# Scores, softmax, transposes and values of two sets of attention tiles as one chain that goes in step

## The chip, the core and the metric

The kernel runs on one core of a Trainium2 chip. The metric is the device time of one execution in microseconds (us), as the median of several executions. The core's engines run side by side, each through its own list of instructions in order: TensorE (PE in the profile, its weight loads PEld), VectorE (DVE), ScalarE (ACT), GpSimdE (POOL) and SyncE (SP), which here issues nearly all DMA commands. They wait for each other by semaphores.

## What is computed

One encoder layer for two sequences with the same weights: A with 1024 rows and B with 512, 1024 features each. All is float32.

```python
u = rmsnorm(x, norm1_g) * (1.0 + sc1) + sh1
z = u @ w_in
z_hy, q, k, v, g = jnp.split(z, ...)
y_hy = hyena_branch(z_hy, ...)        # x0 * long_conv(x1 * v, filter): FFT length 2L
y_at = dilated_attention(q, k, v, ...)
mixed = (g_hy * (y_hy @ w_hy_br) + g_at * (y_at @ w_at_br)) @ w_out
h = x + gt1 * mixed
ff = jnp.square(jax.nn.relu(u2 @ w_up)) @ w_down      # u2: h normalised and modulated
return h + gt2 * ff
```

The shifts, scales and gates (`sh1`, `sc1`, `gt1` and three more) come from a small product with `ada_w`, the modulation. Attention has three groups of four heads of 64 features. A group of dilation 1, 4 or 16 splits the sequence into as many interleaved sub-sequences; a query sees the keys within 64 places on both sides there:

```python
s = jnp.einsum('...bqd,...bkd->...bqk', qb, kw)
s = jnp.where(valid, s + bias, NEG_INF)
m = jnp.max(s, axis=-1, keepdims=True)
p = jnp.exp(s - m)
den = jnp.sum(p, axis=-1, keepdims=True)
o = jnp.einsum('...bqk,...bkd->...bqd', p, vw) / den
lse = (m + jnp.log(den))[..., 0]
```

The three groups' outputs are then merged with weights `softmax(lse)` over the groups.

## The kernel before, in words

**The main stream.** All large products go through `mm3` (matmul on L770): a weight tile of 128 columns against 128 x 512 pieces of the activations, each float32 operand split into a high and a low part, with three products of the parts. Such a product is a *unit*: 48 matmuls for A, 24 for B. `stream` runs the units one after the other: qkv of group 0, zhy (the input of the convolution) third by third mixed with qkv of groups 1 and 2, gates; then the same for B; then the output products (mixA, mixB) and the MLP (ffA, ffB). For each unit the next unit's weights are split (L401 on ACT, L402 on DVE), and a unit's result is evicted from PSUM, for zhy by L1054 on ACT and L1055 and L1056 on DVE. Main products have two PSUM buffers (`psm`); all side work shares four (`pss`).

**Side work.** Everything else is written as generators, *sides*: filters (`filtA`, `filtB`), long convolutions (`conv_gen`, one per third of the channels: L953, L966, a trip through DRAM by L969 and L933, L996, the product with the filter's spectrum, L1007, another trip, L1032), attention (`att_gen`, one per group), the merging of the groups (`combine_gen`, products on L1366), the rest of the modulation (`ada_rest`, L638) and the normalisation of B. A side yields a cost and a latency. After every few main matmuls `pump` adds their cost to a virtual clock and advances whichever started side is ready by it, until the budget, cost times a ratio, is used up. `par` runs several chains of one side together, each with a ready time of its own. So the place of an instruction is decided when the program is built, by numbers, not on the chip. Then a scheduler orders PE, DVE, POOL and SP; ACT keeps the written order. `ada_rest` starts when the three convolutions of A have ended.

**Attention.** `att_gen` waits until q, k and v of its group are there, loads the bias (L1412) and then works tile by tile, a tile being 128 queries. `chain(tiles)` treats one tile, or two where all keys of a tile are 128 (group 2 of A, groups 1 and 2 of B). It has four steps with a yield behind each: scores (L1255 on PE, then scale plus bias L1261 and the row maximum L1264 on DVE), exponentials (L1271 on ACT, with row sums), transposes (L1280 on PE, and the copy of the result by L388), values (L1290 on PE, and a copy into the output). Latencies after the first three are `LSM` = 4.0, `LEX` = 2.5 and `LPT` = 2.5. The chains ran through `par([...], WA)` with `WA` = 2: two at a time, each at its own pace, and a new one is begun when one is done.

## Time and profile before

| | |
|---|---|
| median of 3 runs | 2611.21 us (2610.47 to 2611.28) |
| profiled execution | 2608.41 us, span 2606.6 us |
| granted TensorE clock, mean | 0.996 |
| PE busy | 2551.0 us (98%), 12872 instructions |
| DVE, ACT, POOL busy | 48%, 33%, 6% |

Stages of the profiled execution, roughly: qkv, zhy and gates of A to 849 us, qkv and zhy and gates of B to 1254, mixing of A and B to 1556, MLP of A to 2254 and of B to the end. Attention runs beside the main stream between some 130 and 1130 us. In the profile, a wait is put down to the semaphore event that came last. A row of a timeline gives start, duration, engine, line, operation, output and inputs (numbers of buffers left out), shape and, in brackets, the idle time before it and what ended it.

### The profile page before, as it was taken

How to read it: one execution, taken by the hardware profiler on the slowest of the kernel's cores; microseconds unless marked ns; L12 is line 12 of the kernel's file. 1: busy time of each engine (PE TensorE's matmuls, PEld its weight loads, DVE VectorE, ACT ScalarE, POOL GpSimd, SP SyncE). 2: the span in 40 equal slices, each digit the busy share in tenths (PEclk: the TensorE clock that was granted, in tenths of full speed). 3: DMA queues.
4: the chain of work that ended last, by engine and by line, in shares of the span. 5: the costliest groups of instructions: out<-in, count | busy, mean ns of one | idle time of the engine just before them, and what ended most of it. 6: DMA issues, size and time to landing. Idle time of an engine off the chain costs nothing.

```text
span 2606.6 us, 31910 instructions
## 1 busy us (share of the span) xinstructions
PE 2551.0 (98%) x12872; PEld 2051.2 (79%) x12872; DVE 1249.3 (48%) x1626; ACT 861.3 (33%) x1398; POOL 152.0 (6%) x122
## 2 busy tenths in 40 slices
PE   8999999999999899999999989999999999999999
PEld 4677788787888577787788868888888888888887
DVE  4354443744557745653545563333333333554544
ACT  5544323532522454443432442111211121323232
POOL 0111000000010210000122210000000000000000
PEclk9999999999999999999999999999999999999999
DMA  7455575556665354556754531111111112332323
GB/s 270 142 161 186 178 189 169 152 177 163 210 216 196 131 160 138 160 157 214 249 181 139 170 110 49 42 49 55 49 41 48 57 49 73 130 104 90 103 91 105
DMA packets 136953, 348.95 MB, mean 134 GB/s; under 512 B 18888, under 2 KB 50175, under 8 KB 136678
## 3 DMA queue, kind: packets, MB, share of 16 engines
q1 hardware_dynamic: 136518, 346.13, 41.0%
q8 instruction: 102, 1.67, 0.3%
q0 software_dynamic: 288, 0.79, 0.1%
q14 instruction: 45, 0.37, 0.0%
HBM read 278.58 MB, written 71.16 MB: 134 GB/s over the span
## 4 chain that ended last, share of the span: by engine, by line
PE 69%; DVE 2%; DMA 1%; ACT 1%; issue 1%; POOL 0%; SPq 0%; DVEq 0%; ACTq 0%; POOLq 0%
PE ffA__mm L770 27%; PE ffB__mm L770 13%; PE gateA__mm L770 7%; PE mixA__mm L770 6%; PE zhyB__mm L770 4%; PE qkvB__mm L770 3%; PE mixB__mm L770 2%; PE gateB__mm L770 2%; PE filtB__s L901 0%; DVE mixB__wl L402 0%; PE convB__s L1007 0%; DMA convB__g<-convB__dr 0%; PE attB__s L1290 0%; DMA mixA__g<-zhyA__dr 0%; PE convB__s L996 0%
## 5 line engine op out<-in xcount | busy, mean ns | idle before, releaser
L770 PE MATMUL ffA__mm<-ffA__g,ffA__wh 128*128 128x512 f32 x1024 | 274.1, 389 | 0.0
L770 PE MATMUL ffA__mm<-normA__g,ffA__wh 128*128 128x512 f32 x992 | 265.1, 389 | 0.0
L770 PEld LDWEIGHTS ffA__mm<-ffA__g,ffA__wh 128*128 128x128 f32 x1024 | 192.0, 188 | 40.5 <-issue 0.4
L770 PEld LDWEIGHTS ffA__mm<-normA__g,ffA__wh 128*128 128x128 f32 x992 | 186.2, 188 | 38.7
L1545 DVE SCALAR_TENSOR_TENSOR mixA__g<-ffA__mm,adam,mixA__g 128x1024 f32<-128x1024 f32 x64 | 82.1, 1283 | 190.0 <-PE ffA__mm L770 190.0
L770 PE MATMUL ffB__mm<-ffB__g,ffB__wh 128*128 128x512 f32 x512 | 157.8, 389 | 0.0
L770 PE MATMUL ffA__mm<-ffA__g,ffA__wl 128*128 128x512 f32 x512 | 157.7, 389 | 0.0
L770 PE MATMUL ffB__mm<-normB__g,ffB__wh 128*128 128x512 f32 x496 | 152.7, 389 | 0.0
L770 PE MATMUL ffA__mm<-normA__g,ffA__wl 128*128 128x512 f32 x496 | 152.7, 389 | 0.0
L401 ACT CAST ffA__wh<-ffA__wr 128x1024 fp32r<-128x1024 f32 x63 | 66.3, 1052 | 256.6 <-PE ffA__mm L770 213.6
L1527 DVE SCALAR_TENSOR_TENSOR ffA__g<-ffA__mm,ffA__g 128x1024 f32<-128x1024 f32 x32 | 39.2, 1225 | 222.7 <-ACT ffA__g L1526 222.7
L770 PE MATMUL zhyA__mm<-init__g,zhyA__wh 128*128 128x512 f32 x512 | 145.2, 400 | 0.0
L770 PE MATMUL gateA__mm<-init__g,gateA__wh 128*128 128x512 f32 x480 | 132.0, 394 | 0.0
L770 PE MATMUL mixA__mm<-mixA__g,mixA__wh 128*128 128x512 f32 x424 | 115.3, 392 | 3.1 <-DVE mixA__g L1479 1.9
L770 PE MATMUL qkvA__mm<-init__g,qkvA__wh 128*128 128x512 f32 x416 | 117.0, 399 | 0.0
L770 PEld LDWEIGHTS zhyA__mm<-init__g,zhyA__wh 128*128 128x128 f32 x512 | 94.2, 188 | 23.6 <-issue 5.7
L770 PEld LDWEIGHTS ffB__mm<-ffB__g,ffB__wh 128*128 128x128 f32 x512 | 96.0, 188 | 20.2 <-ACT ffB__g L401 0.2
L770 PEld LDWEIGHTS ffA__mm<-ffA__g,ffA__wl 128*128 128x128 f32 x512 | 96.1, 188 | 20.0
L1526 ACT ACTIVATE ffA__g<-ffA__mm 128x1024 f32<-128x1024 f32 x32 | 32.9, 1029 | 237.7 <-PE ffA__mm L770 237.7
L770 PEld LDWEIGHTS ffA__mm<-normA__g,ffA__wl 128*128 128x128 f32 x496 | 93.1, 188 | 19.3
L770 PEld LDWEIGHTS ffB__mm<-normB__g,ffB__wh 128*128 128x128 f32 x496 | 93.1, 188 | 19.3
L770 PEld LDWEIGHTS gateA__mm<-init__g,gateA__wh 128*128 128x128 f32 x480 | 89.5, 188 | 20.2 <-issue 1.3
(499 smaller groups left out, 4910.4 us busy)
## 6 DMA issues: line engine op xcount, KB each, us to landing
ada__g<-ada SPq DMA_DIRECT2D x32, 512.0 KB
ffA__wr<-w_up SPq DMA_DIRECT2D x32, 512.0 KB
ffA__wr<-w_dn SPq DMA_DIRECT2D x32, 512.0 KB
ffB__wr<-w_dn SPq DMA_DIRECT2D x32, 512.0 KB
ffB__wr<-w_up SPq DMA_DIRECT2D x30, 512.0 KB
filtA__dr<-filtA__g SPq DMA_DIRECT2D x24, 512.0 KB
convA__g<-filtA__dr SPq DMA_DIRECT2D x48, 256.0 KB
init__g<-ada SPq DMA_DIRECT2D x16, 512.0 KB
```

The lines of the kernel that those rows point to most:

```text
L401: A.copy(hi, raw)
L770: T.matmul(ps[:, 512 * c:512 * c + 512], ww[:, sl], xx(k)[:, 512 * c:512 * c + 512], start=k == 0 and p == 0, stop=k == kt - 1 and p == 2)
L1526: A.activation(r, ps[:, :L], AF.Relu)
L1527: V.scalar_tensor_tensor(r, ps[:, :L], 0.0, r, ALU.max, ALU.mult)
L1545: V.scalar_tensor_tensor(S.h(m), ps[:, :L], mod(S, 5, m), S.h(m), ALU.mult, ALU.add)
```

## The change

`chain` now takes two sets of tiles, *parts*, at once. Scores of both are computed, then DVE evaluates both, then the exponentials of both, the transposes part by part, and the values of both. Each step yields the sum of the parts' costs; the latencies behind scores and exponentials are doubled, that behind the transposes stays. `par` is gone here: the next chain begins when the last one has ended. All instructions are the same in number and shape; lines after L1240 move by 17 (L1255 becomes L1264, L1261 L1271, L1264 L1274, L1271 L1283, L1280 L1293, L1290 L1305, L1366 L1383).

```diff
@@ -1237,67 +1237,84 @@
             return k0, k1, [(t0 - k0, n if n < 128 else min(n, k1 - t0), vv) for t0, n, vv in vts if k0 <= t0 < k1]
-        def chain(tiles):
-            k = {i: keys(i) for i in tiles}
-            nk = k[tiles[0]][1] - k[tiles[0]][0]
-            np_ = len(k[tiles[0]][2])
-            w = 256 // len(tiles)
-            slots = [(a, f, i) for a, (i, f) in enumerate((i, f) for i in tiles for f in range(2))]
-            ps = [pss().rearrange("p (a b) -> p a b", b=w) for _ in range(2)]
-            s = [sp.tile([128, 512 // w, w], F32, tag="sc", name=nm("sc"), bufs=4) for _ in range(2)]
-            pieces = k[tiles[0]][2]
-            full = max(o for o, _, _ in pieces) + 128
-            for t in s if full > nk else ():
-                G_.memset(t[:, :, nk:full], 0.0)
-            for a, f, i in slots:
-                k0, k1, _ = k[i]
+
+        class Part:
+            pass
+
+        def chain(parts):
+            subs = []
+            for tiles in parts:
+                c = Part()
+                subs.append(c)
+                c.tiles = tiles
+                c.k = {i: keys(i) for i in tiles}
+                c.pieces = c.k[tiles[0]][2]
+                c.nk = c.k[tiles[0]][1] - c.k[tiles[0]][0]
+                c.np = len(c.pieces)
+                w = 256 // len(tiles)
+                c.slots = [(a, f, i) for a, (i, f) in enumerate((i, f) for i in tiles for f in range(2))]
+                c.ps = [pss().rearrange("p (a b) -> p a b", b=w) for _ in range(2)]
+                c.s = [sp.tile([128, 512 // w, w], F32, tag="sc", name=nm("sc"), bufs=4) for _ in range(2)]
+                full = max(o for o, _, _ in c.pieces) + 128
+                for t in c.s if full > c.nk else ():
+                    G_.memset(t[:, :, c.nk:full], 0.0)
+                for a, f, i in c.slots:
+                    k0, k1, _ = c.k[i]
+                    for hh in range(2):
+                        T.matmul(c.ps[hh][:, a, :c.nk], q(f)[64 * hh:64 * hh + 64, 128 * i:128 * i + 128],
+                                 kx(f)[64 * hh:64 * hh + 64, k0:k1], start=True, stop=True)
+            for c in subs:
                 for hh in range(2):
-                    T.matmul(ps[hh][:, a, :nk], q(f)[64 * hh:64 * hh + 64, 128 * i:128 * i + 128],
-                             kx(f)[64 * hh:64 * hh + 64, k0:k1], start=True, stop=True)
-            for hh in range(2):
-                for a, f, i in slots:
-                    h, k0 = 2 * f + hh, k[i][0]
-                    o = (k0 - 128 * i + 64, k0 - 128 * i + 128, 0)[gi] - x0
-                    V.scalar_tensor_tensor(s[hh][:, a, :nk], ps[hh][:, a, :nk], rq[:, 2 * hh + f, i:i + 1],
-                                           bias[h][:, o:o + nk], ALU.mult, ALU.add)
-                for b, i in enumerate(tiles):
-                    V.tensor_reduce(st[:, i, 2 * hh:2 * hh + 2], s[hh][:, 2 * b:2 * b + 2, :nk], AX.X, ALU.max,
-                                    negate=True)
-            yield 0.0034 * nk * len(tiles) + 0.3, LSM
-            table(LN_EXP)
-            for hh in range(2):
-                for a, f, i in slots:
-                    sl = 2 * hh + f
-                    A.activation(s[hh][:, a, :nk], s[hh][:, a, :nk], AF.Exp, bias=st[:, i, sl:sl + 1],
-                                 accum_out=st[:, i, 4 + sl:5 + sl])
-            yield 0.0, LEX
-            pT = []
-            for hh in range(2):
-                pt = pss().rearrange("p (a b) -> p a b", a=4)
-                pT.append(sp.tile([128, 4, 128], F32, tag="pT", name=nm("pT"), bufs=4))
-                for a, f, i in slots:
-                    for j, (o, _, _) in enumerate(k[i][2]):
-                        T.transpose(pt[:, a * np_ + j], s[hh][:, a, o:o + 128], ident)
-                na = len(slots) * np_
-                copy(pT[hh][:, :na], pt[:, :na])
-            yield 0.22 * np_ * len(slots), LPT
-            po = pss().rearrange("p (a b) -> p a b", a=4)
-            for b, i in enumerate(tiles):
+                    for a, f, i in c.slots:
+                        h, k0 = 2 * f + hh, c.k[i][0]
+                        o = (k0 - 128 * i + 64, k0 - 128 * i + 128, 0)[gi] - x0
+                        V.scalar_tensor_tensor(c.s[hh][:, a, :c.nk], c.ps[hh][:, a, :c.nk],
+                                               rq[:, 2 * hh + f, i:i + 1], bias[h][:, o:o + c.nk], ALU.mult, ALU.add)
+                    for b, i in enumerate(c.tiles):
+                        V.tensor_reduce(st[:, i, 2 * hh:2 * hh + 2], c.s[hh][:, 2 * b:2 * b + 2, :c.nk], AX.X,
+                                        ALU.max, negate=True)
+                del c.ps
+            yield sum(0.0034 * c.nk * len(c.tiles) + 0.3 for c in subs), LSM * len(subs)
+            for c in subs:
+                table(LN_EXP)
                 for hh in range(2):
-                    for j, (_, _, vv) in enumerate(k[i][2]):
-                        for f in range(2):
-                            h = 2 * f + hh
-                            T.matmul(po[64 * f:64 * f + 64, 2 * b + hh], vv[:, 64 * h:64 * h + 64],
-                                     pT[hh][:, (2 * b + f) * np_ + j], start=j == 0, stop=j == np_ - 1)
-            for b, i in enumerate(tiles):
-                n0 = 128 * i
-                t0 = n0 % per * dil + n0 // per
+                    for a, f, i in c.slots:
+                        sl = 2 * hh + f
+                        A.activation(c.s[hh][:, a, :c.nk], c.s[hh][:, a, :c.nk], AF.Exp, bias=st[:, i, sl:sl + 1],
+                                     accum_out=st[:, i, 4 + sl:5 + sl])
+            yield 0.0, LEX * len(subs)
+            for c in subs:
+                c.pT = []
                 for hh in range(2):
-                    copy(O(hh)[:, t0:t0 + 127 * dil + 1:dil], po[:, 2 * b + hh])
-            yield 0.45 * np_ * len(tiles) + 0.3, 0.0
+                    pt = pss().rearrange("p (a b) -> p a b", a=4)
+                    c.pT.append(sp.tile([128, 4, 128], F32, tag="pT", name=nm("pT"), bufs=4))
+                    for a, f, i in c.slots:
+                        for j, (o, _, _) in enumerate(c.k[i][2]):
+                            T.transpose(pt[:, a * c.np + j], c.s[hh][:, a, o:o + 128], ident)
+                    na = len(c.slots) * c.np
+                    copy(c.pT[hh][:, :na], pt[:, :na])
+                yield 0.22 * c.np * len(c.slots), 0.0
+            yield 0.0, LPT
+            for c in subs:
+                c.po = pss().rearrange("p (a b) -> p a b", a=4)
+                for b, i in enumerate(c.tiles):
+                    for hh in range(2):
+                        for j, (_, _, vv) in enumerate(c.k[i][2]):
+                            for f in range(2):
+                                h = 2 * f + hh
+                                T.matmul(c.po[64 * f:64 * f + 64, 2 * b + hh], vv[:, 64 * h:64 * h + 64],
+                                         c.pT[hh][:, (2 * b + f) * c.np + j], start=j == 0, stop=j == c.np - 1)
+            for c in subs:
+                for b, i in enumerate(c.tiles):
+                    n0 = 128 * i
+                    t0 = n0 % per * dil + n0 // per
+                    for hh in range(2):
+                        copy(O(hh)[:, t0:t0 + 127 * dil + 1:dil], c.po[:, 2 * b + hh])
+            yield sum(0.45 * c.np * len(c.tiles) + 0.3 for c in subs), 0.0
         many = 2 if keys(0)[1] == 128 else 1
-        yield from par([chain(range(i, i + many)) for i in range(0, nt, many)], WA)
+        for n in range(0, nt, 2 * many):
+            yield from chain([range(i, i + many) for i in range(n, min(n + 2 * many, nt), many)])
         att_on.remove(gi)
         S.O[gi], S.st[gi] = O, st
```

How the order of instructions moves, at three places. First PE, where conv A's second third (L996, L1007) meets the first tiles of attention's group 1 in A. The names `convA__s` and `attA__s` are results in PSUM. Before:

```order
L996 MATMUL convA__s_3727<-convA__g_3642,convA__cm_3654 128x256 x2
L996 MATMUL convA__s_3734<-convA__g_3642,convA__cm_3654 128x256 x2
L1280 MATMUL attA__s_3772<-csq,attA__sc_3691 128x128 x4
L770 MATMUL zhyA__mm_3755<-init__g_434,zhyA__wh_3592 128x512 x2
L770 MATMUL zhyA__mm_3755<-init__g_430,zhyA__wl_3593 128x512 x2
L1280 MATMUL attA__s_3779<-csq,attA__sc_3692 128x128 x4
L1280 MATMUL attA__s_3792<-csq,attA__sc_3707 128x128 x4
L1280 MATMUL attA__s_3799<-csq,attA__sc_3708 128x128 x4
L1007 MATMUL convA__s_3813<-convA__g_3725,convA__cm_3656 128x256 x2
L1007 MATMUL convA__s_3817<-convA__g_3725,convA__cm_3656 128x256 x2
```

Now:

```order
L1188 MATMUL qkvA__s_3652<-csq,qkvA__g_3605 128x128
L996 MATMUL convA__s_3673<-convA__g_3583,convA__cm_3595 128x256 x2
L996 MATMUL convA__s_3680<-convA__g_3583,convA__cm_3595 128x256 x2
L1264 MATMUL attA__s_3693<-qkvA__g_3371,qkvA__g_3004 128x192
L1264 MATMUL attA__s_3694<-qkvA__g_3371,qkvA__g_3004 128x192
...
L770 MATMUL zhyA__mm_3775<-init__g_253,zhyA__wl_3610 128x512
L1264 MATMUL attA__s_3703<-qkvA__g_3371,qkvA__g_3004 128x256
...
L1007 MATMUL convA__s_3736<-convA__g_3671,convA__cm_3597 128x256 x2
L770 MATMUL zhyA__mm_3775<-init__g_320,zhyA__wh_3609 128x512 x2
L1007 MATMUL convA__s_3740<-convA__g_3671,convA__cm_3597 128x256 x2
```

Before, the last L966 stood 63 main matmuls ahead of the first L996, now 26. The first scores of the group now stand between L996 and L1007, and their transposes (L1293, not in these rows) come 36 to 48 main matmuls behind them, where before transposes (L1280) stood between L996 and L1007.

Second DVE, at the merging of A's groups (L1366, now L1383), which stands beside the start of B's filter and the modulation's multiplies (L638). Before:

```order
L1366 TENSOR_TENSOR attA__g_1375<-combineA__s_7020,attA__g_1375 128x512
L795 TENSOR_SCALAR filtB__g_7001<-filtB__g_7000 128x256
L654 TENSOR_TENSOR qkvB__smt_6973<-qkvB__sma_6971,qkvB__smy_6972 128x16
L638 ISA ada__g_7017,adam<-ada__g_6951,ada__g_5670,prm 128x1024
L638 ISA adam 128x1
L796 TENSOR_SCALAR filtB__g_7001<-filtB__g_7001 128x256
L655 SCALAR_TENSOR_TENSOR qkvB__smt_6973<-qkvB__smt_6973,qkvB__smy_6972 128x16
L638 ISA ada__g_7017,adam<-ada__g_6951,ada__g_5671,prm 128x1024
L638 ISA adam 128x1
L1366 TENSOR_TENSOR attA__g_3845<-combineA__s_7023,attA__g_3845 128x512
```

Now:

```order
L638 ISA ada__g_6897,adam<-ada__g_6822,ada__g_5507,prm 128x1024
L638 ISA adam 128x1
...
L402 TENSOR_TENSOR qkvB__wl_6915<-qkvB__g_6776,qkvB__wh_6914 128x1024
...
L1383 TENSOR_TENSOR attA__g_1450<-combineA__s_6981,attA__g_1450 128x512
...
L1383 TENSOR_TENSOR attA__g_1450<-combineA__s_7022,attA__g_1450 128x512
L795 TENSOR_SCALAR filtB__g_7006<-filtB__g_7005 128x256
L654 TENSOR_TENSOR qkvB__smt_6978<-qkvB__sma_6976,qkvB__smy_6977 128x16
L1383 TENSOR_TENSOR attA__g_3894<-combineA__s_7025,attA__g_3894 128x512
L1383 TENSOR_TENSOR attA__g_5616<-combineA__s_7028,attA__g_5616 128x512
```

The last of the multiplies (L638) stood between merge products; now it stands ahead of all of them, and the merge products of the second piece alternate with rows of the filter.

Third DVE, at group 2 of attention in B; L1055, L1056 and L402 are the main stream's eviction and weight split. Before:

```order
L1055 SCALAR_TENSOR_TENSOR zhyB__g_9011<-zhyB__mm_8933,prm,zhyB__g_9011 128x511
L1261 SCALAR_TENSOR_TENSOR attB__sc_8989<-attB__s_8987,qkvB__rq_7742,attB__g_8941 128x128 x4
L1264 TENSOR_REDUCE attB__st_8940<-attB__sc_8989 128x2 x2
L1261 SCALAR_TENSOR_TENSOR attB__sc_8990<-attB__s_8988,qkvB__rq_7742,attB__g_8941 128x128 x4
L1264 TENSOR_REDUCE attB__st_8940<-attB__sc_8990 128x2 x2
L1056 SCALAR_TENSOR_TENSOR zhyB__g_9011<-zhyB__mm_8933,prm,zhyB__g_9011 128x511
L402 TENSOR_TENSOR zhyB__wl_9018<-zhyB__g_8864,zhyB__wh_9017 128x1024
L1261 SCALAR_TENSOR_TENSOR attB__sc_9036<-attB__s_9034,qkvB__rq_7742,attB__g_8941 128x128 x4
L1264 TENSOR_REDUCE attB__st_8940<-attB__sc_9036 128x2 x2
L1261 SCALAR_TENSOR_TENSOR attB__sc_9037<-attB__s_9035,qkvB__rq_7742,attB__g_8941 128x128 x4
L1264 TENSOR_REDUCE attB__st_8940<-attB__sc_9037 128x2 x2
```

Now:

```order
L1055 SCALAR_TENSOR_TENSOR zhyB__g_9023<-zhyB__mm_8932,prm,zhyB__g_9023 128x511
L1271 SCALAR_TENSOR_TENSOR attB__sc_8977<-attB__s_8975,qkvB__rq_7757,attB__g_8941 128x128 x3
L1274 TENSOR_REDUCE attB__st_8940<-attB__sc_8977 128x2 x2
L1271 SCALAR_TENSOR_TENSOR attB__sc_8978<-attB__s_8976,qkvB__rq_7757,attB__g_8941 128x128 x3
L1274 TENSOR_REDUCE attB__st_8940<-attB__sc_8978 128x2 x2
L1271 SCALAR_TENSOR_TENSOR attB__sc_8989<-attB__s_8987,qkvB__rq_7757,attB__g_8941 128x128 x4
L1274 TENSOR_REDUCE attB__st_8940<-attB__sc_8989 128x2 x2
L1271 SCALAR_TENSOR_TENSOR attB__sc_8990<-attB__s_8988,qkvB__rq_7757,attB__g_8941 128x128 x4
L1274 TENSOR_REDUCE attB__st_8940<-attB__sc_8990 128x2 x2
L1056 SCALAR_TENSOR_TENSOR zhyB__g_9023<-zhyB__mm_8932,prm,zhyB__g_9023 128x511
L402 TENSOR_TENSOR zhyB__wl_9030<-zhyB__g_8880,zhyB__wh_9029 128x1024
```

Each pair of score tiles (L1261 and L1264, now L1271 and L1274) was a group of its own with an eviction and a split between; now the four score tiles of both parts stand between L1055 and L1056 of the same unit.

## The prediction

> **What bounds the kernel now.** I read the page's busy times and chain first, then the matrix engine's waits, then windows and timelines where these waits lie.
>
> ```profile
> PE 2551.0 (98%) x12872; PEld 2051.2 (79%) x12872; DVE 1249.3 (48%) x1626; ACT 861.3 (33%) x1398; POOL 152.0 (6%) x122
> PE 69%; DVE 2%; DMA 1%; ACT 1%; issue 1%; POOL 0%; SPq 0%; DVEq 0%; ACTq 0%; POOLq 0%
> ```
>
> PE is busy for 98% of the span, and its work also makes the chain that ended last. The change issues the same matmuls, so it can win only from the idle 2%, from the gaps between kinds of matmul, and from the clock. The waits of PE that lie near attention, convolution and merging (time in all, count, longest):
>
> ```profile
> PE combineA__s L1364 <- DVE attA__g L1366: 5.4, 2, 3.5
> PE convB__s L1032 <- DMA convB__g<-convB__dr: 2.5, 1, 2.5
> PE qkvB__s L664 <- DVE attA__g L1366: 1.9, 1, 1.9
> PE attA__s L1280 <- ACT attA__sc L1271: 1.7, 1, 1.7
> PE attA__s L1280 <- DVE convA__g L999: 1.7, 1, 1.7
> PE convB__s L996 <- DMA convB__g<-convB__dr: 1.5, 1, 1.5
> ```
>
> Only two of the six name attention's own chain (L1280), 3.4 us together, and the second of them is held by a convolution's product. The others belong to work whose place the change shifts. The windows around three of these places (window, length, busy PE, PEld, DVE, ACT, POOL, granted clock, DMA share, GB/s):
>
> ```profile
> 463.00:475.00 12.00, 8.47 (x48) 6.02 (x48) 11.30 (x17) 8.91 (x24) 0.41 (x2) 0.86 0.17 46
> 877.00:891.00 14.00, 6.55 (x17) 3.01 (x17) 12.70 (x26) 4.80 (x9) 5.63 (x5) 0.75 0.33 112
> 891.00:896.00 5.00, 4.81 (x16) 3.50 (x15) 2.90 (x3) 2.93 (x5) 3.65 (x4) 0.68 0.31 105
> ```
>
> In the first two DVE is busy nearly throughout and PE is not: there DVE's order sets the end. The third has a busy PE at a clock of 0.68.
>
> **The change, part by part.** All matmuls, score passes, exponentials, copies and DMA issues stay; no tile grows. Terms below are in us of the profiled execution.
>
> *Fewer changes between kinds of matmul.* A values or score block stands between streams of main matmuls:
>
> ```profile
> 160.45 0.61 PE L770 MATMUL zhyA__mm<-init__g,zhyA__wl 128*128 128x512 f32 x2
> 161.00 1.97 PE L1290 MATMUL attA__s<-attA__pT,qkvA__g 128*64 128x128 f32 x32
> 163.92 2.58 PE L1255 MATMUL attA__s<-qkvA__g,qkvA__g 64*128 64x256 f32 x16
> 166.43 1.20 PE L770 MATMUL zhyA__mm<-init__g,zhyA__wh 128*128 128x512 f32 x4
> 167.46 0.62 PE L770 MATMUL zhyA__mm<-init__g,zhyA__wl 128*128 128x512 f32 x2
> 167.92 1.09 PE L770 MATMUL zhyA__mm<-init__g,zhyA__wh 128*128 128x512 f32 x4
> ```
>
> Two main matmuls take 0.46 start to start (167.46 to 167.92), thus 0.23 each; before the values block they take 0.55, so 0.09 is lost going in, and the first four after the score block take 1.03 instead of 0.92, so 0.11 coming out. Counted in the order of instructions, PE passes between array shapes 193 times before and 171 times after, since blocks of the two parts now touch: 22 x 0.09 = **-2.0**. Ends: -2.4 (22 x 0.11) and 0, if a block's own first matmul hides it.
>
> *Start of group 1 in A, beside conv A's second third.* Before:
>
> ```profile
> 443.82 0.28 PE L966 MATMUL convA__s<-convA__g,f1ul 128*128 128x256 f32 x1
> 458.77 0.28 DVE L986 COPY convA__g<-convA__g 1x256 f32<-1x256 f32 x1 [10.68 <-DMA convA__g<-filtA__dr]
> 460.09 0.27 DVE L988 MEMSET convA__g<- 1x256 f32 x1 [0.65 <-DMA convA__g<-filtA__dr]
> 467.69 0.93 PE L1280 MATMUL attA__s<-csq,attA__sc 128*128 128x128 f32 x4 [1.75 <-ACT attA__sc L1271]
> 470.34 0.63 PE L1280 MATMUL attA__s<-csq,attA__sc 128*128 128x128 f32 x4 [1.73 <-DVE convA__g L999]
> 470.81 3.50 PE L1007 MATMUL convA__s<-convA__g,convA__cm 128*128 128x256 f32 x8
> ```
>
> The stretch loses 1.75 + 1.73 waiting and some 1.6 in slow matmuls of L1007 (3.50 for eight, where L996 takes 1.89 for eight below). Afterwards L1280's transposes come 36 to 48 main matmuls behind their scores, so both waits and that clock loss go: -5.1. But the convolution's second step (L996) moves from 63 main matmuls behind the last L966 to 26, and the third (L1007) to 40. What its data needs:
>
> ```profile
> 577.89 0.29 PE L966 MATMUL convA__s<-convA__g,f1ul 128*128 128x256 f32 x1
> 588.03 1.89 PE L996 MATMUL convA__s<-convA__g,convA__cm 128*128 128x256 f32 x8
> 1201.07 0.28 PE L966 MATMUL convB__s<-convB__g,f1ul 128*128 128x256 f32 x1
> 1211.64 1.10 PE L996 MATMUL convB__s<-convB__g,convB__cm 128*128 128x256 f32 x4 [1.50 <-DMA convB__g<-convB__dr]
> ```
>
> In A's last third L996 followed after 588.03 - 578.18 = 9.85 with no wait (an upper bound for the way through memory), in B it waited and came after 10.3. Now 26 x 0.23 = 6.0 plus sixteen V transposes (some 1.9) give 7.9: a wait of 0 to 2.4, I take 1.8. Then the product needs the filter spectrum, which DVE got at 460.09, 16.0 after the last L966; L1007 now stands some 13 behind it (40 x 0.23, the transposes, L996, a score block), so it waits for 3 and the product's own length: 4.5 with some clock loss. Together -5.1 + 1.8 + 4.5 = **+1.2**. Ends: -5.1 (loads land earlier, as SP issues them sooner behind the same L969) and +6 (a product of 3 behind it and a clock as at 470.81). Behind a DVE that waits at L986 stand the score passes of both parts and the eviction and weight split of the main stream (L1055, L402).
>
> *Convolution B.* L1032's wait of 2.5 lies behind 25 main matmuls and now 51: 26 more are 6.0, so it goes, **-2.5** (ends -2.5, 0). In its last third L996 moves from 56 to 36 behind L966: 8.3 against 10.3, **+2.0** (0 to 2.7). Conv A's first third goes from 49 to 42: 9.7 against 9.85, **+0.3** (0 to 1.7).
>
> *Group 0 in A.* At one place sixteen transposes and both parts' values now stand without main matmuls between. The copies between them, at the like place before:
>
> ```profile
> 157.04 2.05 ACT L388 COPY attA__pT<-attA__s 128x512 f32<-128x512 f32 x4 [1.67 <-PE attA__s L1280]
> ```
>
> Four copies take 2.05 and the sixteen transposes less, so the second values block waits for about the difference: **+0.7**; ends 0 and 3 (a cast and exponentials queued ahead of the copies).
>
> *The merging of A's groups (L1366, now L1383).* Before:
>
> ```profile
> 879.15 1.28 DVE L638 CUSTOM_DVE_ANT_0 ada__g<-ada__g,ada__g,prm 128x1024 f32<-128x1024 f32 x1
> 880.65 1.28 DVE L638 CUSTOM_DVE_ANT_0 ada__g<-ada__g,ada__g,prm 128x1024 f32<-128x1024 f32 x1
> 882.27 0.68 DVE L1366 TENSOR_TENSOR attA__g<-combineA__s,attA__g 128x512 f32<-128x512 f32 x1
> 883.01 0.49 PE L1364 MATMUL combineA__s<-combineA__g,combineA__g 128*128 128x512 f32 x1 [3.50 <-DVE attA__g L1366]
> 885.37 1.99 PE L1364 MATMUL combineA__s<-combineA__g,combineA__g 128*128 128x512 f32 x3 [1.86 <-DVE attA__g L1366]
> 889.26 1.07 PE L664 MATMUL qkvB__s<-qkvB__g,csq 128*32 128x256 f32 x4 [1.91 <-DVE attA__g L1366]
> 890.26 1.22 PE L770 MATMUL qkvB__mm<-normB__g,qkvB__wh 128*128 128x512 f32 x2
> ```
>
> Of the wait of 3.50, 2 x 1.28 = 2.6 are two multiplies of the modulation (L638) that stand in DVE's order ahead of the product PE waits for. In the new order the last of them stands some fifteen rows before the first merge product, because conv A ends 19 main matmuls (4.3) earlier and that work starts earlier. Also, main matmuls now lie between the merging ones, 11 where 9 merging matmuls stood together: up to 2.5 of cover. 2.6 + about 1.9 of the 2.5 = **-4.5**. Ends: all three waits and the slow clock of 891 to 896, 7.3 + 0.32 x 5 = -8.9; and 0, if the multiplies only stall PE at an earlier place.
>
> [...]
>
> *Bursts in B.* The scores of both parts are now evaluated in one run of DVE:
>
> ```profile
> 1105.56 1.12 DVE L1261 SCALAR_TENSOR_TENSOR attB__sc<-attB__s,qkvB__rq,attB__g 128x128 f32<-128x128 f32 x4
> 1106.59 0.73 DVE L1264 TENSOR_REDUCE attB__st<-attB__sc 128x2 f32<-128x256 f32 x2
> 1108.92 0.74 DVE L1056 SCALAR_TENSOR_TENSOR zhyB__g<-zhyB__mm,prm,zhyB__g 128x511 f32<-128x511 f32 x1
> 1109.58 1.21 DVE L402 TENSOR_TENSOR zhyB__wl<-zhyB__g,zhyB__wh 128x1024 fp32r<-128x1024 f32 x1
> ```
>
> Before, one part (two such pairs, 1108.92 - 1105.56 = 3.4) stood ahead of L1056 and L402; now it is both, 6.8. A unit of B is 24 main matmuls, 5.5, so up to 1.4 of the burst shows in a unit: 1.4 and half of it in another group, **+2.1**. Ends 0 (started early in the unit) and 5 (2 x 1.4 and the split behind it twice, 1.2 each).
>
> *Costed at nothing.* The exponentials of both parts now stand in one row on ACT, whose order is as written:
>
> ```profile
> 151.54 0.45 ACT L1271 ACTIVATE attA__sc<-attA__sc,attA__st 128x192 f32<-128x192 f32 x1
> ```
>
> The second part's four (eight in B) put off the main eviction and cast behind them by at least 4 x 0.45 = 1.8 (3.6). A unit of A lasts 48 x 0.23 = 11 and ACT is busy for a third of the span, so main work covers it; without that cover it costs those 1.8 at each burst that meets an eviction, which the ends of the bursts' and of group 0's terms take in. The chain issues no DMA of its own; its fills on POOL (6% busy) move with the scores, and on SP the bias loads of a group stand behind the convolution's spectrum loads (L984) in both orders, so no queue is passed by anything that PE waits for.
>
> Sum: -2.0 + 1.2 - 2.5 + 2.0 + 0.3 + 0.7 - 4.5 + 2.1 = -2.7, from the profiled 2608.4 (1.8 over its span) to 2605.7. The median of the runs shown lies 2.8 higher, so I expect **2608.5**. A measurement can tell some 0.2% (5.2) from no change: faster is below 2606.0, slower above 2616.4.
>
> **Rivals.** *Merging and group 1 both turn out well* (faster). The merge waits and their clock go entirely (-8.9 instead of -4.5), and the spectrum lands before L1007 (-1.5 instead of +1.2): 2608.5 - 4.4 - 2.7 = **2601.4**. For it speaks that L638 stood right in the way; against it that the waits of 1.86 and 1.91 are for products alone, which remain.
>
> *DVE's queue at group 1* (slower). DVE's wait of 10.68 at L986 was free because nothing due stood behind it. With L996 nearer, the score passes of both parts, the eviction and the split stand behind it, PE's main stream runs dry and the clock falls. It decides once L1007 waits more than about 6. Price: group 1 +9 (three for the spectrum, three for products, 1.6 clock and 1.4 of burst) instead of +1.2, the merge term at -1.5 instead of -4.5, since the multiplies it starts early hit the same queue, and no gain at L1032 in B: 2608.5 + 7.8 + 3.0 + 2.5 = 2621.8 with both of the last two whole, and with half of them, which I take, **2619**. Against it: B's waits of this kind have been 1.5 to 2.5 only.
>
> *The change does nothing*: the stretches only exchange names, switches included: **2611.2**.
>
> **How the numbers follow.** Forecast 0.47, the faster rival 0.29, the slower 0.15, nothing 0.09. The forecast's own range is 2604 to 2613, of which some 0.08 lies below 2606.0 and almost none above 2616.4. Faster: 0.29 + 0.08 = 0.37; slower 0.15; the same 0.48. The range for 8 in 10 goes from the lower half of the faster rival (2599) to short of the slower one's 2619: 2599 to 2618.
>
> **What would show it.** Right: the waits at L1381 below 4 in all and the clock above 0.85 in that stretch; no wait at B's L1032; a new wait of 1 to 3 at L996 in conv A's second third and in conv B's last third; L1280's successor (L1293) without waits at group 1; PE's busy time 1 to 2 lower. Wrong: the modulation's multiplies still right ahead of merge products; a wait over 6 at L1007 or at a main L770 behind L1055; new waits at the values (L1305) of several groups, which would mean that going in step itself costs, by letting both parts wait at once.

## The result: slower by 1.3%, mostly in two places that the prediction had at 2.7 us together

| | before | changed |
|---|---|---|
| median | 2611.24 us (2610.47 to 2614.36, 4 runs) | 2644.52 us (2638.23 to 2648.21, 4 runs) |
| ratio | | 1.0126, 95% interval 1.0114 to 1.0138 |
| profiled execution | 2608.41, span 2606.6 | 2638.23, span 2636.5 |
| mean granted clock | 0.996 | 0.989 |

The forecast was 2608.5, its range 2599 to 2618. The profiled execution of the changed kernel is the shortest of its four, so sums over its trace explain some 30 of the 33 us. The first line of its page (busy times):

```profile
PE 2562.8 (97%) x12872; PEld 2067.7 (78%) x12872; DVE 1250.0 (47%) x1626; ACT 858.9 (33%) x1398; POOL 151.9 (6%) x122
```

As many matmuls as before, yet PE is busy for 11.8 us more: a lower clock makes some of them longer, as rows below show. The other 18 of the 30 us are more idle time. The longest waits of PE beside filter, convolution, attention and merging (time in all, count, longest):

```profile
PE convB__s L1032 <- DMA convB__g<-convB__dr: 8.3, 1, 8.3
PE convB__s L966 <- DVE convB__g L959: 6.7, 3, 5.2
PE filtA__s L881 <- POOL filtA__g L860: 5.0, 3, 1.8
PE attA__s L1264 <- DVE filtA__g L854: 3.9, 1, 3.9
PE combineA__s L1381 <- DVE attA__g L1383: 3.3, 2, 1.9
PE filtA__s L901 <- DMA filtA__g<-filtA__dr: 2.9, 1, 2.9
PE attA__s L1264 <- DVE convA__g L999: 2.7, 1, 2.7
PE convB__s L996 <- DMA convB__g<-convB__dr: 2.7, 2, 2.0
```

The filter's L881 waited before too, in a row that the prediction's list leaves out:

```profile
PE filtA__s L881 <- POOL filtA__g L860: 3.5, 3, 1.7
```

Three names are new at the top: convolution B's first step (L966), the filter's last step (L901), and attention's scores (L1264, twice), held up by products of the filter and of the convolution. Where the time goes, by stages: from the end of one stage's last main matmul (L770 in the timeline of PE) to the end of the next one's, in us of the profiled execution. "A1" is everything up to the end of A's first two thirds of zhy, "A2" goes to the end of its third, "A3" to the end of its gates.

| kernel | A1 | A2 | A3 | qkv B | zhy B | gates B | mix A | rest |
|---|---|---|---|---|---|---|---|---|
| before | 341.5 | 217.1 | 290.6 | 155.9 | 134.9 | 114.0 | 200.2 | 1148.3 |
| changed | 354.1 | 223.0 | 290.2 | 150.6 | 137.6 | 115.6 | 214.6 | 1146.7 |
| difference | +12.6 | +5.9 | -0.4 | -5.3 | +2.7 | +1.6 | +14.4 | -1.6 |

A1 and mix A make 27 of the 30. The start of B, where the groups are merged, gains 5.3, and A2 loses 5.9.

**Place 1: the filter beside attention's group 0 (A1).** DVE (the first three rows) and PE in the changed kernel:

```profile
170.85 0.48 DVE L1271 SCALAR_TENSOR_TENSOR attA__sc<-attA__s,qkvA__rq,attA__g 128x256 f32<-128x256 f32 x1
174.78 1.29 DVE L854 TENSOR_TENSOR filtA__g<-filtA__s,filtA__g 128x512 f32<-128x512 f32 x2 [3.45 <-DMA filtA__g<-c_decay_a]
175.98 0.86 DVE L1271 SCALAR_TENSOR_TENSOR attA__sc<-attA__s,qkvA__rq,attA__g 128x256 f32<-128x256 f32 x2
175.61 2.64 PE L1264 MATMUL attA__s<-qkvA__g,qkvA__g 64*128 64x256 f32 x8 [3.90 <-DVE filtA__g L854]
199.75 1.13 PE L881 MATMUL filtA__s<-filtA__g,csq 128*128 128x256 f32 x4 [1.66 <-POOL filtA__g L860]
203.00 1.94 PE L869 MATMUL filtA__s<-filtA__g,csq 64*64 64x256 f32 x26 [0.25 <-DVE filtA__g L885]
215.65 1.10 PE L901 MATMUL filtA__s<-filtA__g,filtA__cm 128*128 128x256 f32 x4 [2.94 <-DMA filtA__g<-filtA__dr]
```

A filter product on DVE waits 3.45 for its table from memory. It holds side buffers of PSUM, the scores of both parts want all four, and so PE stands for 3.90. (That the buffers are what the scores wait for is inferred from who ends the wait.) Later the filter's steps follow each other closely: L881, then most of L869 in one block, then L901, 2.94 too early for its data. Before, L869 was spread between main matmuls, and L901 came at 213.23 without a wait, 14 us after the last L869:

```profile
193.03 1.09 PE L869 MATMUL filtA__s<-filtA__g,csq 64*64 64x256 f32 x16
195.65 1.09 PE L869 MATMUL filtA__s<-filtA__g,csq 64*64 64x256 f32 x16
198.27 1.09 PE L869 MATMUL filtA__s<-filtA__g,csq 64*64 64x256 f32 x16
213.23 1.02 PE L901 MATMUL filtA__s<-filtA__g,filtA__cm 128*128 128x256 f32 x4
```

**Place 2: the last third of convolution B (mix A).** DVE (first two rows) and PE in the changed kernel:

```profile
1274.82 0.69 DVE L1036 TENSOR_TENSOR convB__g<-convB__s,convB__g 128x512 f32<-128x512 f32 x1 [6.36 <-DMA convB__g<-zhyB__dr]
1275.55 0.68 DVE L959 TENSOR_TENSOR convB__g<-convB__s,convB__g 64x512 fp32r<-64x512 f32 x1
1276.29 0.58 PE L966 MATMUL convB__s<-convB__g,f1uh 128*128 128x256 f32 x1 [5.17 <-DVE convB__g L959]
1280.92 0.41 PE L966 MATMUL convB__s<-convB__g,f1ul 128*128 128x256 f32 x1
1292.28 0.67 PE L996 MATMUL convB__s<-convB__g,convB__cm 128*128 128x256 f32 x2 [1.99 <-DMA convB__g<-convB__dr]
1334.01 1.02 PE L1007 MATMUL convB__s<-convB__g,convB__cm 128*128 128x256 f32 x4
1344.99 3.68 PE L1032 MATMUL convB__s<-csq,convB__g 128*128 128x64 f32 x16 [8.33 <-DMA convB__g<-convB__dr]
```

and PE there before:

```profile
1274.95 0.30 PE L966 MATMUL convB__s<-convB__g,f1uh 128*128 128x256 f32 x1
1278.85 0.28 PE L966 MATMUL convB__s<-convB__g,f1ul 128*128 128x256 f32 x1
1322.57 1.02 PE L1007 MATMUL convB__s<-convB__g,convB__cm 128*128 128x256 f32 x4
1336.91 1.89 PE L1032 MATMUL convB__s<-csq,convB__g 128*128 128x64 f32 x16
```

In the order of PE, 61 main matmuls stood between the transposes of this third (L953) and its first L966, now 24; 52 stood between the last L1007 and the first L1032, now 7. L966 needs DVE's L959, which stands behind L1036, and that waits 6.36 for a load; L1032 needs a trip through memory. Both become waits of PE (5.17 and 8.33), and both are followed by a low clock (0.50, in the last three windows below). Windows of the changed kernel at place 1, at the merge, and at both waits of place 2 (window, length, busy PE, PEld, DVE, ACT, POOL, granted clock, DMA share, GB/s):

```profile
165.00:180.00 15.00, 11.10 (x96) 7.81 (x95) 11.52 (x17) 3.62 (x9) 5.96 (x4) 0.78 0.31 106
892.00:906.00 14.00, 10.39 (x37) 6.89 (x38) 12.40 (x24) 6.53 (x11) 6.10 (x4) 0.88 0.21 75
1266.00:1285.00 19.00, 13.31 (x53) 10.74 (x52) 8.57 (x10) 7.81 (x13) 0.00 (x0) 0.82 0.50 175
1334.00:1350.00 16.00, 7.67 (x32) 6.60 (x31) 5.30 (x5) 6.96 (x8) 2.98 (x1) 0.71 0.78 263
```

These windows hold the waits themselves. The stretches right behind the waits of 3.90, 5.17 and 8.33 alone show half the clock:

```profile
175.60:180.00 4.40, 4.39 (x12) 3.24 (x13) 4.40 (x10) 1.16 (x2) 2.54 (x2) 0.50 0.00 0
1276.30:1281.00 4.70, 4.17 (x16) 3.58 (x17) 2.79 (x4) 3.78 (x6) 0.00 (x0) 0.50 0.27 107
1345.00:1349.00 4.00, 4.00 (x17) 3.91 (x18) 0.00 (x0) 1.07 (x2) 0.00 (x0) 0.50 1.02 409
```

The first L966 behind the wait of 5.17 takes 0.58, where it took 0.30, a later one 0.41 instead of 0.28, and sixteen L1032 take 3.68 behind the wait of 8.33, where they took 1.89. So a wait of PE costs more than its length here.

### The profile page after: what moved, and what is told of

Its sections match the earlier page's. It is cut to its first block, busy times and chain, and to the rows that moved or that the text cites. A ratio compares the mean times of both kernels' runs of the same rounds, so it can differ in the third digit from the quotient of the medians.

```text
span 2636.5 us, 31897 instructions
## 1 busy us (share of the span) xinstructions
PE 2562.8 (97%) x12872; PEld 2067.7 (78%) x12872; DVE 1250.0 (47%) x1626; ACT 858.9 (33%) x1398; POOL 151.9 (6%) x122
## 4 chain that ended last, share of the span: by engine, by line
PE 50%; DVE 1%; DMA 1%; ACT 1%; issue 1%; SPq 0%; DVEq 0%; ACTq 0%
PE ffA__mm L770 26%; PE ffB__mm L770 13%; PE mixA__mm L770 6%; PE mixB__mm L770 2%; PE gateB__mm L770 1%; DMA convB__g<-zhyB__dr 1%; DVE mixB__wl L402 0%; DMA convB__g<-convB__dr 0%; DMA convB__dr<-convB__g 0%; PE convB__s L1007 0%; PE convB__s L996 0%; ACT mixB__wh L401 0%; DVE mixA__g L402 0%; PE convB__s L1032 0%; DVE normA__g L737 0%
## 5 line engine op out<-in xcount | busy, mean ns | idle before, releaser
L770 PE MATMUL ffA__mm<-ffA__g,ffA__wh 128*128 128x512 f32 x1024 | 274.2, 390 | 0.0
L770 PE MATMUL ffA__mm<-normA__g,ffA__wh 128*128 128x512 f32 x992 | 265.2, 389 | 0.0
L770 PEld LDWEIGHTS ffA__mm<-ffA__g,ffA__wh 128*128 128x128 f32 x1024 | 192.0, 188 | 40.5 <-issue 0.4
L770 PEld LDWEIGHTS ffA__mm<-normA__g,ffA__wh 128*128 128x128 f32 x992 | 186.2, 188 | 38.6
L770 PE MATMUL ffA__mm<-ffA__g,ffA__wl 128*128 128x512 f32 x512 | 157.7, 389 | 0.0
L770 PE MATMUL ffB__mm<-ffB__g,ffB__wh 128*128 128x512 f32 x512 | 157.7, 390 | 0.0
L770 PE MATMUL ffA__mm<-normA__g,ffA__wl 128*128 128x512 f32 x496 | 152.8, 389 | 0.0
L770 PE MATMUL ffB__mm<-normB__g,ffB__wh 128*128 128x512 f32 x496 | 152.7, 389 | 0.0
L401 ACT CAST ffA__wh<-ffA__wr 128x1024 fp32r<-128x1024 f32 x63 | 66.1, 1050 | 256.7 <-PE ffA__mm L770 213.7
L770 PE MATMUL zhyA__mm<-init__g,zhyA__wh 128*128 128x512 f32 x512 | 147.4, 407 | 0.0
L770 PE MATMUL gateA__mm<-init__g,gateA__wh 128*128 128x512 f32 x480 | 129.4, 391 | 0.0
L770 PE MATMUL qkvA__mm<-init__g,qkvA__wh 128*128 128x512 f32 x416 | 117.3, 399 | 0.0
L770 PE MATMUL mixA__mm<-mixA__g,mixA__wh 128*128 128x512 f32 x424 | 115.5, 394 | 1.2 <-DVE mixA__g L402 1.2
L770 PEld LDWEIGHTS zhyA__mm<-init__g,zhyA__wh 128*128 128x128 f32 x512 | 95.7, 191 | 23.4 <-issue 5.3
L770 PEld LDWEIGHTS ffB__mm<-ffB__g,ffB__wh 128*128 128x128 f32 x512 | 96.1, 188 | 20.2 <-ACT ffB__g L401 0.2
L770 PEld LDWEIGHTS ffA__mm<-ffA__g,ffA__wl 128*128 128x128 f32 x512 | 96.1, 188 | 19.9
L770 PEld LDWEIGHTS ffA__mm<-normA__g,ffA__wl 128*128 128x128 f32 x496 | 93.1, 188 | 19.3
L770 PEld LDWEIGHTS ffB__mm<-normB__g,ffB__wh 128*128 128x128 f32 x496 | 93.1, 188 | 19.2
L770 PEld LDWEIGHTS gateA__mm<-init__g,gateA__wh 128*128 128x128 f32 x480 | 89.7, 188 | 19.0 <-issue 0.8
```

The costliest lines, as they stand in the source:

```text
L401: A.copy(hi, raw)
L770: T.matmul(ps[:, 512 * c:512 * c + 512], ww[:, sl], xx(k)[:, 512 * c:512 * c + 512], start=k == 0 and p == 0, stop=k == kt - 1 and p == 2)
```

## The experiments

Two theories. **Theory 1**: the change moves other side work in the timetable (costs, latencies, the virtual clock), and filter and convolution steps come up against their transfers; going in step costs nothing by itself. **Theory 2**: going in step costs, by holding all four side buffers and by bursts on DVE.

### One sequence at a time

The changed loop for one sequence, the chains of before (`single`, a copy of the old function) for the other:

```diff
-        for n in range(0, nt, 2 * many):
-            yield from chain([range(i, i + many) for i in range(n, min(n + 2 * many, nt), many)])
+        if S.N == 'A':
+            for n in range(0, nt, 2 * many):
+                yield from chain([range(i, i + many) for i in range(n, min(n + 2 * many, nt), many)])
+        else:
+            yield from par([single(range(i, i + many)) for i in range(0, nt, many)], WA)
```

> Sequence A's attention goes in step as in the change; B's runs as two interleaved chains as before. Theory 1 (the change only shifts the timetable of the other side work, and filter and convolution steps now come up against transfers): the losses seen in A stay (about +18 us by the start of A's gates, of which the merge gives 5 back), while B's stages are as before where their timetable is: about 2624 us (2618 to 2632). Theory 2 (going in step itself costs: score tiles that hold all four PSUM buffers, bursts on DVE): the cost goes by the number of parts in step, 16 of A's 24 tiles-in-pairs and the rest in B, so also 2620 to 2632 here; the two part with the other runs of this batch.

Measured: 2628.06 us, ratio 1.0065 (1.0039 to 1.0091), which both theories allow. The loss is in A1 and A2 (353.2 and 226.0) and, by 5.1, in mix A; the start of B gains 5.8. The same with `'B'`:

> Only B's attention goes in step; A's runs as before. Theory 1: A's stages as before (849 us at the end of its gates within 1 us); in B a loss only if a convolution step lands close behind its transfer again: between 2608 and 2632 us, with any loss at convolution B's steps, not at attention's. Theory 2: a loss of a third of the whole, about 2622 us, at attention B's score blocks between 900 and 1130 us.

Measured: 2626.88, ratio 1.0066 (1.0051 to 1.0081). Each half loses 17 to 18, together about the whole. In the second, A's stages are as before within 0.5 us and most of the loss is at place 2 (mix A 214.4, 14.2 over before); the stage with attention's scores (zhy B) loses 2.7 and B's gates 4.0. That is as theory 1 has it.

### Nothing in step, the timetable shifted a little

The first of these uses the changed chain with a single part, through `par` as before, so that the only difference to the kernel before is that the yield behind the transposes is split in two. The second is the kernel before with one constant changed. The first:

```diff
-        for n in range(0, nt, 2 * many):
-            yield from chain([range(i, i + many) for i in range(n, min(n + 2 * many, nt), many)])
+        yield from par([chain([range(i, i + many)]) for i in range(0, nt, many)], WA)
```

> Nothing goes in step: single chains, two interleaved as before, but written as the changed chain is, so that the transposes yield their cost and their latency apart. That shifts the timetable a little (the order of PE differs in some 1,800 rows). Theory 1: such a shift alone moves the time by several us to tens of us, 2605 to 2635, and the waits that it makes are at filter and convolution steps. Theory 2: within 5 us of before, 2606 to 2616.

Measured: 2621.53, ratio 1.0044 (1.0029 to 1.0059). All of the loss is place 2 (mix A 213.3, the stages before it within 2 of before), with the same two waits at nearly the same lengths:

```profile
PE convB__s L1032 <- DMA convB__g<-convB__dr: 6.8, 1, 6.8
PE convB__s L966 <- DVE convB__g L959: 6.7, 3, 5.2
```

So that loss needs no attention in step. The second:

```diff
-LSM = 4.0
+LSM = 5.0
```

> The kernel before with one number of the timetable changed: the latency behind the scores is 5.0 instead of 4.0. Nothing goes in step. Theory 1: again several us to tens of us either way, 2605 to 2635. Theory 2: within 5 us of before, 2606 to 2616.

Measured: 2616.5, ratio 1.0025 (1.0015 to 1.0035): a small loss from one number, now in B's gates (122.3). The bound of theory 2 (2616) is passed by 0.5 only, less than the noise; the first of the two tells more.

### The two halves of the change apart

Parts in step, latencies as before:

```diff
-            yield sum(0.0034 * c.nk * len(c.tiles) + 0.3 for c in subs), LSM * len(subs)
+            yield sum(0.0034 * c.nk * len(c.tiles) + 0.3 for c in subs), LSM
...
-            yield 0.0, LEX * len(subs)
+            yield 0.0, LEX
```

> The changed kernel with the latencies behind scores and exponentials not doubled (4.0 and 2.5). Still in step, with another timetable. Theory 1 (the timetable against the transfers decides): a clearly different time, outside 2639 to 2649, somewhere in 2610 to 2665. Theory 2 (going in step itself costs): 2639 to 2649.

Measured: 2612.45, ratio 1.0008 (0.9999 to 1.0018). Nearly the whole loss is gone, and theory 2 with it. And the other half alone, in the kernel before:

```diff
-LSM = 4.0
-LEX = 2.5
+LSM = 8.0
+LEX = 5.0
```

> The kernel before, with the latencies behind scores and exponentials doubled (8.0 and 5.0): the other half of the change alone, nothing goes in step. In the order of PE, convolution B's last third stands as in the changed kernel (24 main matmuls ahead of L966, 7 ahead of L1032). If the doubled latencies make the loss: 13 from that third, and filter steps of A bunched as in the changed kernel, 8 to 18 more: 2637 us (2626 to 2645). Rival: they cost only where parts go in step, since with two chains apart the one fills the other's latency: 2606 to 2616.

Measured: 2636.19, ratio 1.0095 (1.008 to 1.011), as forecast. Going in step alone costs some 2 us, which the interval does not tell from nothing, the doubled latencies alone 25, both together 33. The waits of the kernel with the doubled latencies and nothing in step:

```profile
PE convB__s L1032 <- DMA convB__g<-convB__dr: 8.0, 1, 8.0
PE convB__s L966 <- DVE convB__g L959: 6.4, 3, 5.1
PE filtA__s L881 <- POOL filtA__g L860: 4.5, 3, 1.6
PE attA__s L1255 <- DVE convA__g L999: 3.2, 1, 3.2
```

The waits of place 2 and L881's are those of the changed kernel. The 3.90 behind L854 and the 2.94 at L901 are missing, and still A1 takes 351.7, 10.2 over before: those two waits come with parts in step as well, most of the loss of A1 without. One latency doubled alone, in step: first only the second line of the diff above (`LEX` not doubled), then only the first (`LSM` not doubled).

> In step, with only the latency behind the scores doubled. B's last third stands as in the changed kernel: 13 of loss from there. In A the filter's products stand with 16, 24 and 40 main matmuls between steps, two of them as near as in the changed kernel: 3 to 10 more: 2629 us (2622 to 2638). Rival, that each latency has its share by its size (4.0 of 6.5): 2632.

Measured: 2619.37, ratio 1.0032 (1.0019 to 1.0045).

> In step, with only the latency behind the exponentials doubled. B's last third stands as with no latency doubled (47 main matmuls ahead of L966, 54 ahead of L1032), so no loss from there; in A not known, -2 to +8 against no latency doubled: 2614 us (2608 to 2621). Rival by shares (2.5 of 6.5): 2625.

Measured: 2618.82, ratio 1.0032 (1.002 to 1.0043). The stages explain why the first was missed: place 2 came as read from the order (mix A 214.2), A1 lost 4.8, but A2 gained 5.3 (211.8) and B's start 5.6, which I had not counted. Why A2 gained is open. The rival by shares fell too: each latency adds some 7 to the kernel in step without (2612.45), both add 32.

### Place 1

The filter's table loaded one step earlier:

```diff
         def taps(jg):
-            dec = g((4, 256))
-            dma(dec, S.decay[th, jg])
+            dec_load(jg + 1)
+            dec = decs.pop(jg)
             yield 0.0, 3.0
```

> The changed kernel, with the decay table of each filter step loaded one step earlier (one more buffer; no cost or latency changes). If the late transfer, with DVE's queue and the score tiles behind it, makes the loss at the second score block of group 0: its wait of 3.90 and the low clock around it (0.78 over 15 us, 3.3) go, -7: 2637 us (2633 to 2641). Rival: the scores of both parts hold all four side buffers of PSUM and PE waits there for DVE in any case: the wait stays under another name, 2642 to 2646.

Measured: 2646.55, ratio 1.014 (1.0122 to 1.0159); against the changed kernel no gain, and just above the rival's range too. In its trace the wait is what the forecast says:

```profile
172.76 1.72 PE L1273 MATMUL attA__s<-qkvA__g,qkvA__g 64*128 64x256 f32 x8 [1.12 <-DVE filtA__g L863]
```

(lines are 9 later here.) 3.90 became 1.12, and A1 went from 354.1 to 349.8. But A2 is 4.7 and A3 6.5 longer, the latter with a convolution A whose last step now waits five times for its loads. These differences come out too large: by medians the two kernels are 2 us apart, by the profiled executions 12, since one was the slowest of its four and the other the fastest. So the late table is a cause of the wait, and not of the loss as a whole: 8 of A1's loss stayed, and some came elsewhere. Whether the earlier loads brought that or chance did is open. The next one takes the doubled latencies away in A's group 0 only:

```diff
-            yield 0.0, LEX * len(subs)
+            yield 0.0, LEX * (len(subs) if gi or S.N == 'B' else 1)
```

(and `LSM` likewise.)

> The changed kernel with the latencies not doubled in A's group 0 alone. There the filter's steps stand in order nearly as before (taps at 396, 408 and 420 main matmuls, their products apart from 426 to 444, L901 from 474 on). If it is the doubled latencies of group 0 that bunch the filter's steps against their data, the first stage of A is back at 340 to 342 (354.1 in the changed kernel, 341.5 before): 2631 us (2626 to 2636). Rival: it is parts in step that do it there: 2641 to 2648.

Measured: 2624.32, ratio 1.005 (1.0035 to 1.0066): 20 less than the changed kernel, and a little less than the range. A1 is 338.9, below the 341.5 of before, with both parts in step there; by the profiled executions 15 of the gain lie in A1. What group 0's latencies do to the filter, in the order of PE (main matmuls ahead of each step of A's second third):

```
                      L850 (four)          L869 (four of 8)      L901, first
before                372 396 408 420      426 432 438 444       480
in step, not doubled  372 396 408 420      426 432 438 444       480
only doubled          384 395 414 438      445 450 450 450       474
```

The doubled latencies put L850 off and bring most of L869 into one block, 24 main matmuls ahead of L901 instead of 36; in the changed kernel it is 8 (460 and 468).

### Place 2

Earlier loads for the last step of every third, of A and of B; and that step in B's last third held behind the main matmuls written ahead of it, by 12 more latency and by `issue_after`, which keeps its place in the order behind the main matmul last written (`main[0]`):

```diff
-        yield 0.0, 11.0
+        x0s = [g((L,)) for _ in range(2)]
+        for cc in range(2):
+            dma(x0s[cc], S.x0[2 * th + cc])
+        yield 0.0, 11.0 + (12.0 if S.N == "B" and th == 2 else 0.0)
...
-            x0 = g((L,))
-            dma(x0, S.x0[ct])
+            x0 = x0s.pop(0)
...
-                for j8 in range(8):
+                with tc.issue_after(main[0]) if S.N == "B" and th == 2 else ExitStack():
+                    for j8 in range(8):
```

> The changed kernel, with the two inputs that convolution B's last step multiplies with loaded with its other data, ahead of the latency, and with that step in the last third kept behind the main matmuls that are written ahead of it (12 more latency; 67 main matmuls instead of 7 between L1007 and L1032). If the last third's nearness to its transfers makes the loss in mixA: the waits of 5.17 and 8.33 and about 3 of slow clock go, -16: 2628 us (2624 to 2633). Rival: the main stream of mixA waits for its own data there, so the waits only change names: 2640 to 2646.

Measured: 2628.11, ratio 1.0072 (1.0056 to 1.0089): the 16 expected. That the sum comes out to the us is luck in part. Mix A takes 15.9 less than in the changed kernel, as forecast, but the loads moved the other stages as well: A1 5.5 more, A2 9.0 less, B's gates 7.9 more. The same edit in the kernel with nothing in step:

> The same two edits in the kernel in which nothing goes in step and the transposes yield apart (2621.5 us). It has the same waits there, 5.22, 2.44 and 6.78, and no other loss against the kernel before. If they are its whole loss: 2608 us (2604 to 2612). Rival as above: 2618 to 2624.

Measured: 2610.05, ratio 0.9997 (0.9988 to 1.0007). In both, mix A is back (198.7 and 198.6); B's gates take some 6 to 8 more (123.5 and 121.0), where L1032 of the other thirds now waits:

```profile
PE convB__s L1037 <- DMA convB__g<-convB__dr: 4.3, 2, 2.4
```

(of the first of the two; L1032 is L1037 there.) Both places mended at once, by this edit and that of group 0:

> Both edits together in the changed kernel: no doubled latencies in A's group 0 (alone -20) and the mended last step of convolution B (alone -16). If these two places are all of the loss of 33 they add up: 2609 us (2605 to 2613). Rival: they overlap, or a third place takes over when the rest runs earlier: 2613 to 2622.

Measured: 2613.45, ratio 1.0012 (1.0003 to 1.0022). 31 of the 33 are gone, where the two edits alone gave 20 and 16: so they overlap a little, as the rival has it. A1 and mix A are back (339.6 and 200.2), 29 less than in the changed kernel. Of the other stages A2 takes 6.4 less, A3 2.7 and B's gates 7.5 more. (The profiled executions are only 24 apart, since that of the changed kernel was its fastest.)

### Is there a version that beats both?

In step without doubled latencies (the diff above), with the mending of place 2, L1007 of that third held back in the same way:

> In step without doubled latencies, with the loads and the order of convolution B's last step as mended before. Its waits in B's convolution were 2.8 and 1.6 at L996 and 3.5 and 1.3 at L1007, which these edits do not take away, so little is to be had: 2611 us (2606 to 2615). If it beats both kernels, it is because the earlier loads let DVE finish sooner.

Measured: 2617.99, ratio 1.0026 (1.0016 to 1.0037), outside the range and 5.5 slower than without the mending: place 2 gains 3.8 (mix A 200.5 instead of 204.3), B's gates lose 12.9 (127.9 instead of 115.0).

One sequence in step without doubled latencies, the other with the chains of before (the loop of the first diff); first A:

> Only A in step and without doubled latencies; B as before, and in the order of PE its convolution stands where it stood before (61 main matmuls ahead of L966 and 52 ahead of L1032 in the last third). By stages: A as in the kernel in step without doubled latencies (-1.7, +2.4, +1.8 to the end of the gates, -6.3 in B's first products with the merge), B's later stages as before: 2607 us (2603 to 2610). It beats both kernels if so. Rival: B shifts by these 4 us against its transfers, though not in order, and loses them: 2610 to 2614.

Measured: 2610.53, ratio 0.9998 (0.9989 to 1.0007): no gain. A1 (-2.4) and the merge (qkv B -4.7) won 7.1 of the 8.0 forecast, but A2 and A3 took 6.5 of it back (+4.3, +2.2; 4.2 expected), and mix A lost 4.6 with its convolution in the old order. Most of that loss stands behind a wait that the kernel before has too. Here, and before:

```profile
1255.51 7.06 PE L1032 MATMUL convB__s<-csq,convB__g 128*128 128x64 f32 x32 [2.52 <-DMA convB__g<-convB__dr]
1256.62 3.76 PE L1032 MATMUL convB__s<-csq,convB__g 128*128 128x64 f32 x32 [2.53 <-DMA convB__g<-convB__dr]
```

The granted clock over these matmuls was 1.00 before; sixteen of them took 3.68 at the 0.50 of the changed kernel (at 1344.99), so by an estimate from these times it was about 0.5 here. So part of a difference of a few us can be the clock, behind one and the same wait. Then B:

> Only B in step and without doubled latencies; A as before. Convolution B stands as in the kernel in step without doubled latencies (47 and 54 main matmuls in the last third, but L996 and L1007 of its second half together): mixA 4 longer, zhyB and gates 2 longer, the rest as before: 2616 us (2611 to 2620).

Measured: 2612.9, ratio 1.0009 (1.0 to 1.0018). I found no version that is measurably faster than the kernel before.

## Why the prediction was wrong, point by point

- **The step that failed.** The terms of group 0 in A (+0.7) and of convolution B's last third (+2.0) failed, and with them the choice of what to price. I looked where PE waited before (the six waits) and asked what the change does there. For these places the terms were near. But a change that moves work can make a wait at any place that had slack, and such a place may have no row among the waits of before. The filter did have one (L881, 3.5 in three waits), and I left it out. "It can win only from the idle 2%" is right; nothing bounds the loss.
- **The signs were chosen at the same places.** Most signs of being right came true: the waits at L1381 are 3.3 in all at a clock of 0.88, L996 waits at both places named, L1293 waits nowhere, and L1032's old wait is gone. Yet the time was 36 us above the forecast. Only PE's busy time, 11.8 up instead of 1 to 2 down, and the new wait at B's L1032 told against it.
- **"Group 0 in A": +0.7, end 3.** A1 lost 12.6. I read sixteen transposes and two values blocks there, and not that most of L869 stood there as one block, with L881 ahead of it and L901 8 main matmuls behind it. The order showed all of this. Runs: undoing the doubled latencies of this group alone brings A1 to 338.9.
- **"Convolution B, in its last third": +2.0.** L996 waited 1.99, as worked out. But I checked only L996 of the third's three distances. L966 (24 instead of 61) waited 5.17, L1032 (7 instead of 52) 8.33; with the clock, mix A lost 14.4. The row of the second third's L1032 (2.5, gone as forecast) was in my list, and I did not apply it to the last third.
- **Start of group 1: +1.2.** From the start of the 1153rd main matmul to the end of the 1440th it took 129.1 us instead of 126.4: +2.7. L996 waited 1.17 (I took 1.8), but the wait is put down to a copy on ACT (L388) and not to its load. The wait for the spectrum showed not at L1007 but at the second scores (L1264, 2.74). It ends with the convolution's product on DVE (L999), so the scores probably wanted a side buffer that this product held. L1293 waits nowhere, as said.
- **Convolution A, first third: +0.3.** L996 did not wait. A2 lost another 3.2 ahead of the 1153rd main matmul, which itself waited 1.85 for a cast of weights (L401 on ACT). I had not looked for that.
- **The merge: -4.5.** B's first stage gained 5.3; the two waits at L1381 are 1.91 and 1.38, the clock 0.88 instead of 0.75. Parts in step without doubled latencies gain 6.3 there (149.6), and the doubled latencies alone 4.1 (151.9), so the gain is not tied to going in step.
- **Bursts in B: +2.1.** zhy B lost 2.7. The agreement may be luck: with the doubled latencies alone, and so without double bursts, it lost 3.9 (138.8).
- **Fewer changes between array shapes: -2.0.** Not separated by any run; PE's busy time rose by 11.8 instead, at a mean clock of 0.989 where it was 0.996.
- **The slower rival** had a DVE queue at L986 and 2619. Its place was wrong: DVE did wait there for 8.40 (10.68 before), and it cost little.

The doubled latencies had a line of their own in the change, and I gave them no term: they move every other piece of side work. The runs show them to be worth 25 alone and 32 in step, of the 33.

Three waits here were followed by a lower clock: behind those of 3.90, 5.17 and 8.33 the granted clock was 0.50 over the 4.4, 4.7 and 4.0 us of the windows above. What decides it is not shown. The length of a wait alone does not: behind one of 2.53 the 32 matmuls of L1032 took 3.76 before, at a clock of 1.00, and behind one of 2.52 at the same place they took 7.06 with only A in step.

## What to carry to other kernels

Where a program's order comes from a timetable, read a change to one of its numbers as a change to everything that follows: list every producer and consumer with a trip through memory between them, count the work between them before and after, and compare it with the longest trip that the trace shows (here 11 us from the end of L966 at 1281.33 to L996 at 1292.28, some 48 main matmuls of 0.23), not only at the places that wait already. Test a structural change apart from the numbers that come with it: here the structure was nearly free and two factors of two alone cost 1%. And a kernel whose timetable has been tuned should be compared with itself under a shifted timetable first: here one split yield cost 0.44%, five times the 0.08% of going in step.

## What was not expected of the hardware

Waits of PE were dearer than their length: in the 15 us around one of 3.90 the granted clock was 0.78, in the 16 us around one of 8.33 it was 0.71, and sixteen small matmuls took 3.68 instead of 1.89. Nor does the length of a wait decide it: behind waits of 2.52 and 2.53 at the same place the same 32 matmuls took 7.06 in one kernel and 3.76 in the other.
